# Fifteen small loads, of 1 to 15 rows, put beside a saturated load stream

## The chip, the cores and the metric

One core of one Trainium2 chip. The metric is the device time of one execution, in microseconds (us). A program on one core is timed in several runs; the profile comes from one more execution. Its "span" runs from the first to the last instruction and is some 1.8 to 2.1 us shorter than the device time.

## The reference, cut to what matters

```python
# B, S, D, W = 4, 4096, 4096, 64;  x is (4, 4096, 4096) fp32, w is (4096, 4096) fp32
def reference(x, w, offsets):
    for b in range(B):
        o = int(offsets[b])
        results.append(x[b, o:o+W] @ w)          # four windows of 64 rows, one weight matrix
    return np.stack(results).astype(np.float32)   # (4, 64, 4096)
```

The weights are 67.1 MB of fp32 and the windows 4.2 MB. Every byte is read once: 71.3 MB.

## The kernel before

POOL (GpSimd) issues nearly all loads, as its queue can turn fp32 into fp16 on the way. The weights come in blocks of up to four times 128 rows into three rotating buffers `wc`, then in a "tail" of 1 MB pieces (counted as fp16):

```python
blocks = [(0, 1), (1, 1), (2, 4), (6, 4), (10, 4), (14, 4), (18, 3), (21, 3)]
k_tail = 24
wc_pool = ctx.enter_context(tc.tile_pool(name="wc", bufs=3))
x_pool = ctx.enter_context(tc.tile_pool(name="xp", bufs=1))
...
for k0, r in blocks[2:]:
    t = wc_pool.tile([P, R_MAX * N], fp16, name="wc", tag="wc")
    nc.gpsimd.dma_start(
        out=t[:, : r * N],
        in_=w[k0 * P : (k0 + r) * P, :].rearrange("(p r) n -> p (r n)", r=r),
    )
```

For each block PE multiplies all eight column groups for both pairs of windows, and DVE adds each result to the accumulator; the program is in manual order, so each engine runs its instructions as they are written:

```python
whole_rows([0, 1], range(8), True)
for k0, r in blocks[2:-1]:
    whole_rows(range(k0, k0 + r), range(8), False)
```

At the end the second half of the output goes out through two hardware queues, ACT's and SP's. SP does nothing between its one load at the start and these stores:

```python
q = [nc.scalar, nc.sync]
for h in range(2):
    ...
    for g in range(G):
        for j in js:
            add_out(4 * g + j, g, ng * n_sub + j)
        store(q[g], g, c0, c0 + NG // 2)
```

## Time and profile before

| | before |
|---|---|
| time, median of 2 runs | 182.29 us (182.23 to 182.35) |
| span of the profiled execution | 180.6 us |
| share of the span on the chain that ended last | DMA 63%, PE 26% |
| bytes read | 71.30 MB |
| last load of weights landed, PE starts its last pieces | 164.84 us |

How to read it: the chain says that the end was waiting for data for most of the time, and the bytes read, over the time in which they were read, say at what rate. The lines, with their reading, stand in the prediction.

### The profile page before, as it was taken

How to read it: one execution, taken by the hardware profiler on the slowest of the kernel's cores; microseconds unless marked ns; L12 is line 12 of the kernel's file. 1: busy time of each engine (PE TensorE's matmuls, PEld its weight loads, DVE VectorE, ACT ScalarE, POOL GpSimd, SP SyncE). 2: the span in 40 equal slices, each digit the busy share in tenths (PEclk: the TensorE clock that was granted, in tenths of full speed). 3: DMA queues.
4: the chain of work that ended last, by engine and by line, in shares of the span. 5: the costliest groups of instructions: out<-in, count | busy, mean ns of one | idle time of the engine just before them, and what ended most of it. 6: DMA issues, size and time to landing. Idle time of an engine off the chain costs nothing.

```text
span 180.6 us, 1505 instructions
## 1 busy us (share of the span) xinstructions
PE 125.7 (70%) x576; PEld 58.1 (32%) x576; DVE 80.5 (45%) x120; ACT 16.5 (9%) x23; POOL 14.5 (8%) x29
## 2 busy tenths in 40 slices
PE   0000779504999399808995699999399999987900
PEld 0000774101444144303442244444044444433400
DVE  0000657500578278802876168899374000820460
ACT  2412446500000000000000000000000000400000
POOL 4600000000000100000001000050500100020000
PEclk9999999965799999996999889999879999999996
DMA  5999989999999899999989989999999999999994
GB/s 178 321 256 212 281 181 196 236 232 232 225 218 218 174 210 234 236 218 232 210 181 203 245 191 245 194 239 196 191 212 213 215 216 214 212 216 206 370 419 196
DMA packets 4952, 40.98 MB, mean 227 GB/s; under 512 B 466, under 2 KB 466, under 8 KB 3282
## 3 DMA queue, kind: packets, MB, share of 16 engines
q0 software_dynamic: 4080, 36.70, 93.8%
q1 hardware_dynamic: 432, 2.10, 3.2%
q10 hardware_dynamic: 434, 2.10, 2.8%
q8 instruction: 4, 0.07, 0.1%
q14 instruction: 2, 0.02, 0.0%
HBM read 71.30 MB, written 4.19 MB: 418 GB/s over the span
## 4 chain that ended last, share of the span: by engine, by line
DMA 63%; PE 26%; issue 3%; DVE 2%; POOL 1%; POOLq 1%; DVEq 0%
DMA wc<-in_w_dram 63%; PE bank L144 26%; DVE acc L154 2%; POOL wc L108 1%; POOLq L70 1%; POOL xrow L77 0%; DVEq L251 0%; POOL identity masks.py:197 0%; POOLq L77 0%; POOL w L66 0%; POOLq masks.py:199 0%; DVEq L154 0%; POOLq L240 0%
## 5 line engine op out<-in xcount | busy, mean ns | idle before, releaser
L144 PE MATMUL bank<-wc,xT 128*128 128x512 f16 x480 | 111.6, 396 | 26.2 <-DMA wc<-in_w_dram 26.2
L154 DVE TENSOR_TENSOR acc<-acc,bank 128x512 f32<-128x512 f32 x100 | 67.0, 686 | 70.7 <-PE bank L144 70.0
L144 PEld LDWEIGHTS <-xT 128*128 128x128 f16 x512 | 51.5, 101 | 93.1 <-DMA wc<-in_w_dram 26.7
L130 PE MATMUL bank<-identity,xrow 128*128 128x128 f16 x64 | 7.1, 312 | 20.0 <-DMA xrow<-in_x_dram 20.0
L139 DVE CAST xT<-bank 128x512 f16<-128x512 f32 x8 | 5.5, 692 | 21.9 <-PE bank L130 21.9
L130 PEld LDWEIGHTS <-xrow 128*128 128x128 f16 x64 | 6.7, 149 | 20.2 <-issue 20.2
L200 ACT COPY tmp<-bank 128x512 f32<-128x512 f32 x4 | 2.1, 600 | 119.9 <-PE bank L144 119.9
L89 POOL DMA_DIRECT2D wc<-in_w_dram x6 | 3.2, 542 | 88.2 <-PE bank L144 88.2
L108 POOL DMA_DIRECT2D wc<-in_w_dram x10 | 6.7, 683 | 36.0 <-PE bank L144 26.4
L144 PE MATMUL bank<-w,xT 128*128 128x512 f16 x32 | 7.2, 382 | 0.0
L169 DVE COPY acc<-bank 128x512 f32<-128x512 f32 x8 | 5.5, 692 | 1.4 <-PE bank L144 1.2
L141 ACT CAST xT<-bank 128x512 f16<-128x512 f32 x8 | 4.7, 586 | 8.2 <-PE bank L130 8.2
L171 ACT COPY acc<-bank 128x512 f32<-128x512 f32 x8 | 4.7, 586 | 2.3 <-PE bank L144 2.3
L189 POOL DMA_DIRECT2D out_dram<-acc x2 | 1.1, 534 | 18.1 <-DVE acc L205 18.1
L205 DVE TENSOR_TENSOR acc<-acc,tmp 128x512 f32<-128x512 f32 x4 | 2.5, 681 | 0.0
L63 ACT CAST w<-acc 128x2048 f16<-128x2048 f32 x1 | 1.9, 1897 | 4.9 <-DMA acc<-in_w_dram 4.9
L77 POOL DMA_DIRECT2D xrow<-in_x_dram x4 | 2.1, 523 | 2.1 <-issue 2.1
L62 ACT CAST w<-acc 128x2048 f16<-128x2048 f32 x1 | 1.9, 1897 | 3.0 <-DMA acc<-in_w_dram 3.0
L62 ACT ACT_TABLE_LOAD x1 | 1.3, 1283 | 1.8 <-PEq L240 1.8
L66 POOL DMA_DIRECT2D w<-in_w_dram x1 | 0.7, 660 | 0.8 <-POOLq L240 0.8
masks.py:199 POOL TENSOR_SCALAR_AFFINE_SELECT identity<-identity 128x128 f16<-128x128 f16 x1 | 0.3, 287 | 0.1
masks.py:197 POOL MEMSET identity<- 128x128 f16 x1 | 0.2, 223 | 0.0
(4 smaller groups left out, 0.4 us busy)
## 6 DMA issues: line engine op xcount, KB each, us to landing
wc<-in_w_dram POOLq DMA_DIRECT2D x4, 4096.0 KB, 48.2
wc<-in_w_dram POOLq DMA_DIRECT2D x7, 1024.0 KB, 27.5
wc<-in_w_dram POOLq DMA_DIRECT2D x2, 3072.0 KB, 36.1
xrow<-in_x_dram POOLq DMA_DIRECT2D x4, 512.0 KB, 14.7
out_dram<-acc POOLq DMA_DIRECT2D x2, 1024.0 KB, 14.5
acc<-in_w_dram SPq DMA_DIRECT2D x1, 1024.0 KB, 5.3
w<-in_w_dram POOLq DMA_DIRECT2D x1, 1024.0 KB, 12.2
acc<-in_w_dram ACTq DMA_DIRECT2D x1, 1024.0 KB, 11.5
```

Of the source, the lines that this page charges most:

```text
L62: nc.scalar.copy(out=w_one[0][:, :NG], in_=w0_32[:, :NG])
L77: nc.gpsimd.dma_start(out=x16[g][m * WIN : (m + 1) * WIN, :], in_=x[b][bass.ds(o, WIN), :],)
L89: nc.gpsimd.dma_start(out=t[:, : r * N], in_=w[k0 * P : (k0 + r) * P, :].rearrange("(p r) n -> p (r n)", r=r),)
L108: nc.gpsimd.dma_start(out=t[:, pos : pos + n * wd].rearrange("p (t n) -> p t n", t=n), in_=w[ki * P : (ki + n) * P, ng * NG + c0 : ng * NG ...
L130: nc.tensor.matmul(out=ps[t][:, i * P : (i + 1) * P], lhsT=x_cols(g, 4 * t + i), rhs=identity[:], start=True, stop=True,)
L139: nc.vector.tensor_copy(out=dst, in_=ps[t][:])
L141: nc.scalar.copy(out=dst, in_=ps[t][:])
L144: nc.tensor.matmul(out=ps[bank][:], lhsT=xT[g][:, kt * P : (kt + 1) * P], rhs=rhs, start=start, stop=stop,)
L154: nc.vector.tensor_add(out=dst, in0=dst, in1=ps[bank][:])
L169: nc.vector.tensor_copy(out=acc[g][:, c * NT : (c + 1) * NT], in_=ps[bank][:])
L171: nc.scalar.copy(out=acc[g][:, c * NT : (c + 1) * NT], in_=ps[bank][:])
L205: nc.vector.tensor_add(out=dst, in0=dst, in1=tmp[2 * g + j // 2][:])
```

## The change

Its intent, as far as the code tells it: to see what a handful of tiny transfers, issued from an otherwise idle queue in the middle of a saturated stream, costs. The loaded data are used by nothing. Each load has n rows of 16 fp32 numbers, 64 bytes a row, for n from 1 to 15. The memset before them, on DVE, is what holds them in place: SP waits for it.

```diff
     tmp = [acc_pool.tile([P, NT], fp32, name=f"tmp{i}") for i in range(4)]
+    small = x_pool.tile([16, 16 * 16], fp32, name="small")
     acc = [acc_pool.tile([P, N], fp32, name=f"acc{g}") for g in range(G)]
 ...
     for k0, r in blocks[2:-1]:
         whole_rows(range(k0, k0 + r), range(8), False)
+        if k0 == 10:
+            nc.vector.memset(small[:], 0.0)
+            for n in range(1, 16):
+                nc.sync.dma_start(
+                    out=small[:n, 16 * n : 16 * n + 16], in_=w[0:n, 16 * n : 16 * n + 16]
+                )
```

## The prediction

> **What bounds the kernel now.** I read the page first, then the chain that ended last, then busy time by stretches, then the two timelines where the change lands. The page of the profile, its parts 1 to 4:
>
> ```profile
> span 180.6 us, 1505 instructions
> ...
> DMA  5999989999999899999989989999999999999994
> ...
> q0 software_dynamic: 4080, 36.70, 93.8%
> q1 hardware_dynamic: 432, 2.10, 3.2%
> q10 hardware_dynamic: 434, 2.10, 2.8%
> ...
> HBM read 71.30 MB, written 4.19 MB: 418 GB/s over the span
> ...
> DMA 63%; PE 26%; issue 3%; DVE 2%; POOL 1%; POOLq 1%; DVEq 0%
> ```
>
> The span is 180.6 us of the 182.29 us measured. The DMA row stands at 8 or 9 tenths in every slice but the first and last. Of the packet time, 93.8% of 16 engines' span is queue 0, the loads and two stores that POOL issues; the two hardware queues (q1 is SP's, q10 is ACT's) have 6% between them. The chain is 63% DMA. The chain of waits in order of time, from the middle on:
>
> ```profile
> 59.54 41.55 DMA wc<-in_w_dram
> ...
> 101.13 26.05 PE bank L144 x112
> ...
> 127.47 1.39 POOL wc L108 x2
> 128.86 35.94 DMA wc<-in_w_dram
> ...
> 164.84 5.36 PE bank L144 x24
> 170.20 1.35 DVE acc L154 x3
> ```
>
> Columns are start, length, what. PE's 26.05 us from 101.13 is there only because the chain stepped to the buffer that PE freed for the last loads. The following 35.94 us of DMA say the same thing as the total: 71.30 MB are read from 0.9 us to the landing at 164.8 us, 71.30 MB / 163.9 us = 435 GB/s. After that landing come 7 us of matmuls, the adds and the stores, which wait for nothing else. Busy time by stretch shows whether the stream ever runs dry:
>
> ```profile
> core 0: us, PE busy (x) PEld busy (x) DVE busy (x) ACT busy (x) POOL busy (x), PEclk, DMA share, GB/s
> 43.00:97.00 54.00, 45.44 (x192) 19.49 (x192) 32.06 (x47) 0.00 (x0) 1.06 (x2) 0.93 1.00 215
> 98.00:101.00 3.00, 0.00 (x0) 0.00 (x0) 0.10 (x1) 0.00 (x0) 0.20 (x1) 1.00 0.72 153
> 108.00:127.00 19.00, 19.00 (x89) 8.53 (x87) 17.07 (x27) 0.00 (x0) 2.83 (x4) 1.00 1.02 218
> 133.00:163.00 30.00, 29.34 (x137) 13.24 (x136) 9.46 (x15) 2.06 (x4) 2.16 (x4) 1.00 1.06 214
> ```
>
> The last two columns are the DMA share and GB/s written into SBUF; the loads read fp32 and write fp16, so what is read is twice that: 430, 436 and 428 GB/s in the three long stretches. One rate through blocks in long pieces and the tail in short ones: the DMA engines are the wall. The 0.72 in the three-microsecond stretch is no hole: packets of 2.4 us are counted where they start, and the neighbouring microseconds make up for it (97 to 98 us alone counts 1.82). Anything that takes time on the busiest of the 16 DMA engines before 164.8 us moves the end; anything on SP, and short work in a gap of DVE, does not.
>
> **What the Trainium skill says, and whether this trace agrees.**
> (1) "DMA: Bandwidth & Descriptors", Issuing engines are not separate DMA queues: loads issued by any engine run on the same 16 DMA engines and interleave. Agrees: two loads of the same 1024 KB, one from SP and one from ACT, were issued 0.5 us apart and took 5.3 and 11.5 us to land.
> (2) The same page, Why a DMA increments its semaphore by 16 and not by 1: a hardware load is spread over the largest k of at most 16 that divides the slowest dimension of both sides, on the lowest-numbered k engines, each writing one completion. So n rows (n from 2 to 15) would use engines 0 to n-1. The trace has one small load to compare, the offsets on ACT's queue. SP's queue has 432 packets: three transfers of 128 rows and 3 x 16 completions. ACT's has 434, the same and two more: one data packet, one completion, so k = 1. The case n = 11 or 13 no run shows yet.
> (3) The same page, Queues, rings and completion order: an engine takes turns between its queues a packet at a time, and a completion write lands only after all earlier writes of that engine, whatever their queue. The first half agrees with the interleaving in (1). What the second half costs the other queue is the rival below.
> (4) "HBM Reference", Latency: an access takes 0.2 us on average, 2 us under high load. I use it only to size that rival; the trace of before does not show it by itself.
>
> **The change part by part.** It removes nothing. It adds one memset, fifteen loads on SP's queue, and a buffer of 1 KB per partition, used by nothing that is computed. The order on each engine is the program's own, so the memset comes after the sixteen adds of the block that starts at 10 and before those of the next. The timeline there:
>
> ```profile
> 97.41 0.69 DVE L154 TENSOR_TENSOR acc<-acc,bank 128x512 f32<-128x512 f32 x1 [0.18 <-PE bank L144]
> 97.67 0.53 POOL L89 DMA_DIRECT2D wc<-in_w_dram  x1 [20.55 <-PE bank L144]
> ...
> 101.13 4.33 PE L144 MATMUL bank<-wc,xT 128*128 128x512 f16 x12 [3.76 <-DMA wc<-in_w_dram]
> 102.21 0.69 DVE L154 TENSOR_TENSOR acc<-acc,bank 128x512 f32<-128x512 f32 x1 [4.11 <-PE bank L144]
> ```
>
> *The memset.* The last add of that block ends at 97.41 + 0.69 = 98.10 us, and DVE then stands idle for 4.11 us until the first group of the next block. An add of 512 columns takes 0.69 us on DVE; half the columns, 256, at no better pace is 0.34 us (an estimate). It fits twelve times over: cost 0. POOL's issue of the next block load at 97.67 is through at 98.20, 0.1 us into the memset, and the data it calls for is queued behind a whole block anyway.
>
> *Issuing on SP.* What SP does in the whole kernel, by its timeline:
>
> ```profile
> 0.87 0.38 SPq L59 DMA_DIRECT2D acc<-in_w_dram  x1
> 172.08 2.72 SPq L189 DMA_DIRECT2D out_dram<-acc  x2
> ```
>
> Between 0.87 and 172.08 us it does nothing. At the 0.38 us that its one load took to issue, fifteen are 5.7 us: from about 98.5 to 104.2 us if nothing holds them. The framework may make later ones wait for the landing of earlier ones, to use a completion counter again. In the worst case every data packet and every completion waits for one turn behind a packet of the big stream: 30 turns. The trace's own packet records give 2.43 us for the packets of four-row blocks and 1.83 us for those of three-row blocks. Four turns to about 109 us, ten to 128 us, and the rest behind the tail's packets of 0.32 us: all done before 135 us. SP is needed at 172. Cost 0.
>
> *The DMA engines.* 1 + 2 + ... + 15 = 120 rows of 64 bytes, 7.7 KB beside 71.3 MB: the bytes are nothing. The packets count. With k = n, engine 0 gets fifteen data packets and fifteen completions, engine 14 one of each, engine 15 none. In the packet records, the 32-byte packet of the offsets took 7 ns, and a completion 9 ns on SP's queue and 22 ns (median) on POOL's. A data packet of 64 bytes I put at 7 to 14 ns (an estimate). Engine 0: 15 x (7 + 9) = 0.24 us to 15 x (14 + 22) = 0.54 us. The wc landings wait for the slowest engine; if that is engine 0, the end moves by this, otherwise by less, down to 0.
>
> *The end.* SP's closing waits may have some more completion counters to look at, all long reached: I allow 0.1 us. The new buffer moves the addresses of those after it by 1 KB; nothing in the profile depends on that.
>
> Sum: 0 + 0 + (0 to 0.54) + (0 to 0.1) us, so 0 to 0.64, middle 0.3: 182.6 us.
>
> **The rivals.**
> *Wholly hidden.* Engine 0 is not the slowest, and its delay is absorbed by the lag of another. For it: the skill's count puts all the load on low engines. Against: the views don't show single DMA engines. Time 182.3, which cannot be told from my own number without many rounds.
>
> *A bubble at each completion or each change of queue.* If an engine had to let its earlier writes land, with nothing else under way, before each of fifteen completions, engine 0 would lose about 0.2 us each by (4): 15 x 0.2 = 3 us, and the time 185.3; at the 2 us of a loaded memory it would be 30 us and 212. Against it: the tail's loads have one completion per sixteen packets on each engine, and POOL's issues that waited for their landings (130.42, 135.32, 140.37 us) are 4.90 and 5.05 us apart, while sixteen packets of 0.324 us are 5.18 us. So a completion leaves no hole in its own queue. Also, while ACT's 1 MB load and POOL's first loads share the engines, the packet records add up to 434 GB/s read, not less than POOL's queue alone (427). What speaks for it: all these were large packets, and fifteen tiny ones on one engine are not seen anywhere in before. I give it 6% for more than 3.65 us.
>
> *SP's queue backs up into its last stores.* Worked out above: it would have to last 74 us, over twice the worst case. Under 1%.
>
> *Faster.* Nothing is removed and no wait is broken; a gain could only be chance.
>
> **Range and chances.** Before ran at 182.23 and 182.35, its profiled execution at 182.56: 0.2 us of noise around a shift of 0 to 0.64. That gives 182.1 to 183.2; I stretch the upper end to 183.8 for small bubbles (0.1 us times fifteen on engine 0). Two per cent is 3.65 us, six times my largest sum, so the verdict is the same with 0.93; slower 0.06 by the bubbles, faster 0.01.
>
> **What would show it right or wrong.** In the changed profile: SP's queue with 120 more data packets and 120 completions, so about 672 packets in place of 432 (fewer if k is smaller for some); the memset on DVE just after 98 us inside an idle gap; the first matmul of the next block still near 101.1 us; fifteen SP issues from about 98.5 us; a last wc landing at 164.8 to 165.5 us; from there to the end some 16 us as before. Wrong if that landing is 3 us or more later with the DMA share in 98 to 135 us lower than 0.97 (bubbles), if a wait of SP for its own small loads reaches 172 us (backing up), or if the matmuls after 101 us wait longer for wc with no later bytes.

## The result, and the profile after

The changed kernel took 182.57 us (182.4 to 182.74, 2 runs) against 182.29 us; the ratio is 1.0011, with a 95% interval of 0.9991 to 1.0031. "Same" was right, and the 182.6 of the prediction too; what has to be found out is whether it was right for its reasons, as 0.28 us is not more than the noise.

The page of the changed kernel, the parts that answer to those shown of before:

```profile
span 180.9 us, 1525 instructions
...
DMA  5999988999999899999998989898999999999994
...
q0 software_dynamic: 4080, 36.70, 93.7%
q1 hardware_dynamic: 672, 2.11, 3.3%
...
HBM read 71.31 MB, written 4.19 MB: 417 GB/s over the span
...
DMA 60%; PE 27%; issue 3%; DVE 2%; another core or an unknown queue 2%; POOL 1%; POOLq 1%; DVEq 0%
```

SP's queue q1 went from 432 to 672 packets: 240 more, 120 rows and 120 completions, as the rule of one engine per row has it, for 11 and 13 as for the rest. POOL's queue is as it was, packet for packet. In the chain of waits in order of time (start, length, what), the end is this:

```profile
116.26 10.55 PE bank L145 x48
...
128.49 36.41 DMA wc<-in_w_dram
...
164.94 5.35 PE bank L145 x24
170.29 1.35 DVE acc L155 x3
```

PE takes up the last pieces at 164.94 us, against 164.84 before. The timeline where the change lands (start, length, engine, line, operation, with the idle time before it in brackets):

```profile
97.42 0.69 DVE L155 TENSOR_TENSOR acc<-acc,bank 128x512 f32<-128x512 f32 x1 [0.17 <-PE bank L145]
...
98.10 0.27 DVE L178 MEMSET small<- 16x256 f32 x1
98.40 27.23 SPq L180 DMA_DIRECT2D small<-in_w_dram  x15
...
101.11 13.99 PE L145 MATMUL bank<-wc,xT 128*128 128x512 f16 x64 [3.72 <-DMA wc<-in_w_dram]
102.18 0.69 DVE L155 TENSOR_TENSOR acc<-acc,bank 128x512 f32<-128x512 f32 x1 [3.81 <-PE bank L145]
```

The memset starts in the nanoseconds in which the last add ends, and DVE still has 3.81 us of idle time after it; the block's first matmul starts at 101.11 us, against 101.13. The surprise is the SP line: fifteen issues stretch over 27 us, from 98.40 to 125.6. Its waits, and the first 5 us of the same timeline cut off at 103 us:

```profile
SPq L196 <- DVE acc L155: 44.7, 2, 42.8
SPq L180 <- DMA small<-in_w_dram: 22.4, 7, 4.3
SPq L258 <- DMA out_dram<-acc: 4.5, 4, 1.2
SPq L196 <- DMA small<-in_w_dram: 3.7, 1, 3.7
```

```profile
98.40 2.59 SPq L180 DMA_DIRECT2D small<-in_w_dram  x8
```

The columns of the first are total us, times, longest. Eight loads go out in a row, 2.59 us; each of the other seven waits for an earlier small load to land, 22.4 us in all. So there are eight completion counters for this purpose, used in turn. This will matter at the end. The last line is SP's first store, which waits 3.7 us for the counter of a small load, straight after the last issue: that is over by about 129.4 us, 40 us before SP is needed, so the prediction's sign of backing up didn't show.

Why does a load of at most 15 rows need 4 us and more? The trace's DMA records (no view prints them singly) show the first data packet at 103.1 us, its completion at 104.9, the next load's data at 106.8, and so on, mostly 1.81 to 1.83 us apart on one engine: one packet, data or completion, for each turn behind a packet of the big stream, which took 1.83 us in this block. (Near 114 and 128.7 us, where the stream goes over to its next load, some come close together.) The last small packet started at 132.6 us. This is the worst case of the prediction's paragraph on SP, and it is what happened; the 40 us to SP's store at 172 were enough.

### The profile page after: what moved, and what is told of

It is laid out like the page before. It is cut to its first block, busy times and chain, and to the rows that moved or that the text cites. A ratio compares the mean times of both kernels' runs of the same rounds, so it can differ in the third digit from the quotient of the medians. Undisturbed runs are those within 1.5% of the kernel's fastest.

```text
span 180.9 us, 1525 instructions
## 1 busy us (share of the span) xinstructions
PE 127.7 (71%) x576; PEld 58.4 (32%) x576; DVE 80.8 (45%) x121; ACT 16.5 (9%) x23; POOL 14.5 (8%) x29
## 4 chain that ended last, share of the span: by engine, by line
DMA 60%; PE 27%; issue 3%; DVE 2%; another core or an unknown queue 2%; POOL 1%; POOLq 1%; DVEq 0%
DMA wc<-in_w_dram 60%; PE bank L145 27%; DVE acc L155 2%; POOL wc L109 1%; POOLq L71 1%; POOL xrow L78 0%; DVEq L258 0%; POOL identity masks.py:197 0%; POOLq L78 0%; POOL w L67 0%; POOLq masks.py:199 0%; DVEq L155 0%; POOLq L247 0%
## 5 line engine op out<-in xcount | busy, mean ns | idle before, releaser
L145 PE MATMUL bank<-wc,xT 128*128 128x512 f16 x480 | 113.4, 400 | 24.5 <-DMA wc<-in_w_dram 24.5
```

The lines of the kernel that those rows point to most:

```text
L145: nc.tensor.matmul(out=ps[bank][:], lhsT=xT[g][:, kt * P : (kt + 1) * P], rhs=rhs, start=start, stop=stop,)
```

## The experiments

Twelve kernels were run, in three calls, each call with its own runs of before on the same chip: 4 to 6 runs of each, 9 to 11 of before. Medians, with ratios:

| run | this, us | before, us | ratio | 95% interval |
|---|---|---|---|---|
| same_again | 182.61 | 182.26 | 1.0014 | 1.0001 to 1.0027 |
| memset_only | 182.34 | 182.26 | 1.0000 | 0.9988 to 1.0012 |
| four_times | 183.08 | 182.26 | 1.0039 | 1.0026 to 1.0052 |
| rows_127 | 182.43 | 182.26 | 1.0003 | 0.9990 to 1.0016 |
| loads_57 | 182.65 | 182.44 | 1.0017 | 1.0003 to 1.0030 |
| loads_12 | 182.75 | 182.44 | 1.0016 | 1.0002 to 1.0030 |
| wide_127 | 193.10 | 182.44 | 1.0615 | 1.0560 to 1.0669 |
| wide_128 | 183.20 | 182.44 | 1.0045 | 1.0030 to 1.0061 |
| loads_17 | 182.32 | 182.33 | 1.0000 | 0.9987 to 1.0014 |
| both_127 | 184.39 | 182.33 | 1.0117 | 1.0102 to 1.0133 |
| mid_127 | 185.09 | 182.33 | 1.0153 | 1.0139 to 1.0166 |
| late60 | 195.98 | 182.33 | 1.0749 | 1.0733 to 1.0766 |

All gave the correct result.

### First call: is there a shift, and is it the packets?

**same_again** is the changed kernel unedited.

> The changed kernel once more, in five rounds, to narrow the shift. Three theories of what the fifteen loads cost. PACKETS: each small packet takes its own recorded time (24 ns for 64 bytes, 22 ns for a completion) from the stream of engine 0, and engine 0 sets the end: 15 x 46 ns = 0.69 us, ratio 1.004. HIDDEN: engine 0 has slack, or the small packets fit into time the stream doesn't use: ratio 1.000. BUBBLE: each completion or change of queue also leaves a hole, 0.1 us or more each: 15 x 0.1 = 1.5 us or more, ratio 1.008 or more.

1.0014, with an interval that just leaves out 1.000: a shift of about a quarter of a microsecond, a third of what the small packets' recorded times add up to on engine 0. BUBBLE is out: a hole of even 0.1 us per completion would be six times the shift. Between PACKETS and HIDDEN it doesn't decide.

**memset_only**:

```diff
         if k0 == 10:
             nc.vector.memset(small[:], 0.0)
-            for n in range(1, 16):
-                nc.sync.dma_start(...)
```

> The memset and the buffer stay, the fifteen loads are left out. All theories: 182.3 us as before, ratio 1.000 within 0.2%, as the 0.27 us of the memset lie in a DVE gap of 4 us. If the shift of the change is found here again, it came from the memset or the moved addresses and not from the loads.

1.0000. The memset and the moved addresses cost nothing; what shift there is belongs to the loads.

**four_times**:

```diff
-            for n in range(1, 16):
+            for i in range(60):
+                n = i % 15 + 1
                 nc.sync.dma_start(
-                    out=small[:n, 16 * n : 16 * n + 16], in_=w[0:n, 16 * n : 16 * n + 16]
+                    out=small[:n, 16 * i : 16 * i + 16], in_=w[0:n, 16 * i : 16 * i + 16]
                 )
```

(and `small` with 64 x 16 columns.)

> Sixty loads in place of fifteen, same shapes, same place. PACKETS: 60 x 46 ns = 2.8 us, 185.1 us, ratio 1.015. HIDDEN: 182.3 to 182.6, ratio below 1.003. BUBBLE: 6 us or more, ratio 1.03 or more. Turns: if engine 0 gives each small packet one turn behind a packet of the big stream, as the records of the changed kernel suggest (a small packet every 1.82 us on engine 0 while the stream moves 1.83 us packets), 120 turns are 16 of 1.83 us and 104 of about 0.35 us: the last small packet near 165 us, just before SP's last stores at 172, so no backing up.

0.82 us by the medians: between PACKETS and HIDDEN, and near neither. The last small completion started at 159.4 us, expected near 165, and SP's stores were issued at 172.17, as with fifteen loads: no backing up. But in the chain of waits PE takes up its last pieces at 164.94 us, exactly as in the changed kernel with fifteen. The stream doesn't know of the 45 further loads. So the 0.4 us that sixty cost over fifteen in the span (181.3 against 180.9) arise after the stream, and I looked there; this is where the theory CLOSING of the second call comes from.

**rows_127**:

```diff
-            for n in range(1, 16):
-                nc.sync.dma_start(...)
+            nc.sync.dma_start(out=small[:127, 0:16], in_=w[0:127, 0:16])
```

(and `small` with 128 partitions.)

> One load of 127 rows of 64 bytes in place of the fifteen: by the skill's rule 127 has no divisor of at most 16 but 1, so all 127 data packets and one completion should lie on one engine; then SP's queue shows 432 + 128 = 560 packets. PACKETS: 127 x 24 ns = 3.0 us, 185.3 us, ratio 1.017. HIDDEN: 182.3 to 182.6. BUBBLE by completion: one hole, 182.5; BUBBLE by change of queue: 127 x 0.1 = 13 us or more. Turns: at one packet a turn the load ends near 165 us; if several of its rows go in one turn, far earlier.

The queue's line on the page, and the chain of waits:

```profile
q1 hardware_dynamic: 560, 2.11, 3.3%
```

```profile
128.82 35.76 DMA wc<-in_w_dram
...
164.62 5.35 PE bank L145 x24
```

560 packets: 127 rows and one completion, so one engine carried them all. They came one per turn, mostly 308 ns apart in the tail of the stream, up to 160.6 us. By their records 2.97 us of that engine's time; measured, 0.17 us by the medians, not clear of noise, and a PE that takes up its last pieces sooner than in before.

The end alone doesn't say whether the packets cost nothing or whether that engine had time in hand; the stream's own completion records do. (The records don't number the engines; "engine 0" is here a name for the one that carries the small load.) In the tail an engine finishes its share of a 1 MB piece every sixteen large packets, and its completion is recorded. In before these completions are 4.895 us apart, on most engines alike. In rows_127 those that stand among the small packets are 4.960 us apart, seventeen small packets between two of them (133.33, 138.29, 143.25 us and so on): 3.8 ns for a small packet, 0.49 us for 127. PACKETS is out: a record's 24 ns is not time taken from the stream. And engine 0 does have time in hand: it finishes the piece before these first of the sixteen, at 128.37 us, when the last one finishes at 129.78. A piece counts as landed with the last engine, so the first 1.4 us that engine 0 loses can't show.

### Second call: the closing waits, and real bytes

After the last store SP goes through the completion counters one after the other before the kernel may end. No view prints these waits singly; the trace's instruction records do. Their starts in us, on SP:

```
before        174.85 174.92 174.98 175.04 175.10 | 175.97 177.23 178.48 179.72 |                                    end 180.61
fifteen       175.00 175.06 175.12 175.19        | 176.25 177.48 178.73 179.82 | 179.88 179.94                      end 180.86
sixty         175.11 175.17                      | 177.84 179.09 180.02        | 180.08 180.14 180.20 180.29 180.37  end 181.28
```

The middle group ends as a store lands; the left ones had been satisfied before, the right ones too, but they are only looked at after the last landing. Each takes 60 to 90 ns of SP. What SP waited for in this phase can be seen in its waits (total us, times, longest) of the sixty loads; the same line of the changed kernel, L258 above, has four waits with a longest of 1.2:

```profile
SPq L259 <- DMA out_dram<-acc: 4.9, 4, 2.6
```

The order is that of the eight counters, and the counter of a store is set by how many hardware loads came before it. Seven hardware transfers in before use seven of them, and the last store has the last. Every load more moves the four stores on by one. With N loads added, the waits left behind the last landing should be, for N = 1, 9, 17, 57: none; for 15: two; for 12 and 60: five.

**loads_57** and **loads_12** are four_times with `range(57)` and `range(12)`.

> The sixty loads less the last three: 57. Theory CLOSING (new, from the traces so far): the loads don't slow the stream at all; they turn the order in which SP's closing waits go through the eight completion counters of hardware loads. A wait that comes after the last store's landing costs about 62 ns; the changed kernel has 2 of them behind the landing, the sixty loads 5, before and the 127 rows none. With 57 loads (57 = 8 x 7 + 1, the place of the single load of 127 rows) none should be left behind: 182.3 to 182.5, ratio below 1.002, where sixty took 1.0039. Theory PACKETS (a cost per small packet, some 12 ns of the 46 seen): 57/60 of the sixty's 0.71 us: 182.95, ratio 1.0037.

> Only the first twelve loads (1 to 12 rows). CLOSING: 12 = 8 + 4, the same place as sixty, so five waits of 62 ns or more behind the landing: 182.6 to 182.9, ratio 1.002 to 1.0035, at least as much as the fifteen (1.0014). PACKETS: 12 x 12 ns = 0.15 us, 182.4, ratio 1.0008, less than the fifteen.

By the clock the two are alike, 1.0017 and 1.0016 (0.21 and 0.31 us by the medians), though the one has almost five times the loads of the other: a cost per load doesn't give that. But 12 came out just under the ratio I gave. And 57, for which CLOSING leaves nothing, took 182.65 us where 182.3 to 182.5 were expected (before itself took 182.44); its ratio is under the 1.002 I gave, but its interval leaves out 1.000. So CLOSING isn't all of the shift there, and the clock can't put the two in order. The trace is sharper. Taken from it, for every run, the time from the end of SP's last store packet to the end of the span:

| waits behind the landing | runs: us |
|---|---|
| 0 | before 1.26, memset_only 1.26, rows_127 1.28, loads_57 1.28, loads_17 1.27, mid_127 1.25, wide_127 1.25, wide_128 1.27 |
| 2 | changed kernel 1.40, same_again 1.39 |
| 5 | loads_12 1.58, four_times 1.63, late60 1.64 |
| 7 | both_127 1.68 |

Fourteen executions, in order, without an exception: 1.25 to 1.28 us, and 60 to 75 ns more for each wait. It doesn't go with the number of loads: twelve loads stand with sixty, 57 with none.

**wide_127** and **wide_128**:

```diff
-            for n in range(1, 16):
-                nc.sync.dma_start(...)
+            nc.sync.dma_start(out=small[:127, :], in_=w[0:127, 0:512])     # wide_127
+            nc.sync.dma_start(out=small[:128, :], in_=w[0:128, 0:512])     # wide_128
```

(and `small` as 128 x 512.)

> One load of 127 rows of 2048 bytes, all on engine 0 as the 127 small rows were. About 80 ns a row (half of the 159 ns that 4096 bytes take in the store's records), so 10.2 us of engine 0's time. If the 3 us of 127 small packets vanished because engine 0 had slack against the other engines, the end moves by 10.2 less that slack: up to 7 us, 189, ratio 1.04. If they vanished because small packets fit into time that the engine doesn't use between the stream's packets, real bytes will not: the full 10 us, 192.5, ratio 1.056. If neither (the end isn't set by the engine that ends last), 182.5.

> One row more: 128 rows of 2048 bytes, so by the skill's rule spread over all sixteen engines, 8 rows each: 8 x 80 ns = 0.64 us on each engine, 182.9, ratio 1.0035, whichever engine sets the end; SP's queue with 432 + 128 + 16 = 576 packets. If the rule of k doesn't hold, the same as 127 rows.

The chain of waits of the two, first 127 rows, then 128:

```profile
129.02 45.37 DMA wc<-in_w_dram
...
174.43 5.35 PE bank L145 x24
```

```profile
130.12 35.31 DMA wc<-in_w_dram
...
165.47 5.35 PE bank L145 x24
```

One row more, and the end comes 9 us sooner. 127 rows sit on one engine, and PE takes up the last pieces at 174.43 us, 9.6 us later than before. (Their 260 KB are 9.8 us at the expectations' 26.5 GB/s, which is 8 KB in 309 ns; in the tail of before an engine starts one every 307.) The time was 192.04 to 194.81 us in four runs; the profiled one is of the faster kind, and why the others took 2 us more I can't say. 128 rows are spread: 0.64 us were expected, PE is 0.63 us later, the time 0.76. That 9.6 is so close to 9.8 us is not a sign that engine 0 has no slack: its completions are now 6.429 us apart, 90 ns more for each small packet, 11.5 us for 127 rows if all cost that (an estimate). Some 1.9 us of it didn't reach the end, about the lead seen in rows_127. The 64-byte packets of rows_127 vanished because they were 0.5 us of work and not 3 us, and because the lead covers that.

### Third call: how small is free, the order of counters again, and the case that hurts

**loads_17** is four_times with `range(17)`.

> Seventeen loads, the fifteen and two more of 1 and 2 rows: 17 = 8 x 2 + 1, the place of 57 and of the single load. CLOSING: no closing wait is left behind the last store's landing, so from that landing's last packet to the span's end about 1.27 us as before, against 1.40 us with fifteen: two loads more, an end 0.13 us sooner; the time 182.3 to 182.6, ratio below 1.0015 (0.13 us is too little for the clock of five rounds to show; the trace decides). PACKETS or BUBBLE: a little more than fifteen.

182.32 against 182.33 us, ratio 1.0000: two loads more than the changed kernel and, if anything, sooner, though the interval is as wide as the shift that is looked for. The trace has no closing wait behind the landing and 1.27 us to the end.

**both_127**:

```diff
+            nc.sync.dma_start(out=small[:127, 0:16], in_=w[0:127, 0:16])
+            nc.scalar.dma_start(out=small[:127, 16:32], in_=w[0:127, 16:32])
```

(in place of the fifteen.)

> The 127 rows of 64 bytes twice, once from SP and once from ACT, both after the memset, so two more queues take turns on engine 0: 254 data packets, 254 x 24 ns = 6.1 us by their records; by their bytes 254 x 64 = 16 KB at the 26.5 GB/s at which the engine moves 8 KB packets, 0.6 us. If the small packets of one queue were hidden in some slack of a few us, twice as many should come out of it: up to 3 us, ratio 1.017. If a small packet costs only its bytes: 182.5 to 183.2, ratio 1.001 to 1.004.

```profile
128.23 38.00 DMA wc<-in_w_dram
...
166.27 5.35 PE bank L145 x24
```

2.06 us. CLOSING has its part: this pair leaves seven waits behind the landing, 0.42 us. PE takes up the last pieces 1.43 us later than in before, which neither the bytes (0.6 us) nor the records (6.1 us) give. The records show what happened turn by turn: on each turn of engine 0 one packet of each of the two queues, and turns of 331 ns (median, after 131 us) where rows_127 with one packet per turn had 308. Without any small packet, a 1 MB piece of the tail, sixteen turns per engine, landed every 4.90 and 5.05 us: 306 and 316 ns a turn. So the first small packet of a turn hardly lengthens it (3.8 ns, as above), the second adds some 20 ns, near its recorded time. By the completions of engine 0, 5.309 us apart, a pair costs 24 ns, 3.1 us for 127 pairs (an estimate, as above); less the lead of 1.4 us or somewhat more, that is about what PE shows. My expectation that one rule would hold for both was wrong.

**mid_127** is rows_127 with 128 columns, 512 bytes a row.

> 127 rows of 512 bytes on engine 0, between the 64 bytes that cost nothing to be seen and the 2048 bytes that cost 10.7 us. By bytes: 127 x 512 / 26.5 GB/s = 2.45 us, 184.8, ratio 1.013. By their share of what 2048 bytes cost, 10.7 / 4 = 2.7 us, ratio 1.015. If a piece up to some size fits into unused time of the engine, clearly less than 2 us, ratio below 1.010.

```profile
129.04 38.55 DMA wc<-in_w_dram
...
167.63 5.36 PE bank L145 x24
```

2.76 us, PE 2.8 us later: 22 ns a row, a little over the 19 ns of its bytes (127 x 512 bytes are 2.45 us). But here too the lead of engine 0 hides a part: its completions are 5.469 us apart, 34 ns for each small packet, 4.3 us for 127. Put together ("hidden" is the estimated loss less what PE shows):

| 127 rows on engine 0 | its loss per row (or pair), ns | times 127, us (estimate) | PE later than before, us | hidden, us |
|---|---|---|---|---|
| 64 bytes | 3.8 | 0.5 | -0.2 | all |
| 64 bytes, twice | 24 | 3.1 | 1.4 | 1.7 |
| 512 bytes | 34 | 4.3 | 2.8 | 1.5 |
| 2048 bytes | 90 | 11.5 | 9.6 | 1.9 |

So two things are at work: a lone 64-byte packet in a turn costs next to nothing, and whatever engine 0 loses, some 1.5 to 1.9 us of it is covered by the slower engines. What sizes between 64 and 512 bytes cost wasn't measured.

**late60** moves the memset and sixty loads behind the adds of the first output half:

```diff
+    nc.vector.memset(small[:], 0.0)
+    for i in range(60):
+        n = i % 15 + 1
+        nc.sync.dma_start(
+            out=small[:n, 16 * i : 16 * i + 16], in_=w[0:n, 16 * i : 16 * i + 16]
+        )
     ng = order[1]
     k_fine = n_k - n_fine
```

(and the block at `k0 == 10` goes; `small` has 61 x 16 columns.)

> The sixty loads moved to the end: the memset after the last adds of the first output half (near 159 us), the loads on SP from there, in front of SP's last two stores. The rival of the prediction that I gave under 1%: SP's queue backing up into its stores. Sixty loads landing one per 0.4 to 1 us, with eight completion counters, keep SP until 185 to 200 us, where its first store was issued at 172; the end comes some 8 us after that: 192 to 208, ratio 1.05 to 1.14. If SP doesn't hold its stores back behind its loads' landings, or they land much faster near the end: 182.5 to 185.

SP's timeline, and one line of its waits:

```profile
0.87 0.38 SPq L60 DMA_DIRECT2D acc<-in_w_dram  x1
159.04 29.73 SPq L212 DMA_DIRECT2D small<-in_w_dram  x60
188.89 0.85 SPq L190 DMA_DIRECT2D out_dram<-acc  x2
```

```profile
SPq L212 <- DMA small<-in_w_dram: 5.2, 9, 1.6
```

The sixty take SP from 159.04 to 188.8 us, about 0.5 us each, and its two stores, issued from 172.08 in before, leave at 188.89. The end is 13.65 us later. PE takes up its last pieces at 164.64 us, so the stream is as fast as ever. The same sixty loads cost 0.8 us in the middle and 13.7 at the end. The number came out as expected, the reason only in part: waits for small loads to land make up 5.2 us of the 29.7, one more wait for a store 3.2 us. Most of it is the issuing itself, 0.295 us a load (median) and what lies between.

## Why the prediction was right or wrong

**The total and the verdict** were right: 182.57 for 182.6, "same" at 0.93.

**What bounds the kernel** was right and is now shown: some 11 us of work on one DMA engine (wide_127) moved the end by 10.7 us; the memset and SP's issuing, off the engines, moved nothing that was measured.

**The memset, SP's issuing, the turns** were right: memset 0.27 us for an estimated 0.34, in the gap named; an issue 0.30 us (median) for 0.38; 672 packets; all small packets gone by 132.6 us for "before 135". The loads did not go out by 104 us; they ran into the worst case that the text had set aside beside it, and its sum held (its first four turns took 1.83 us and not 2.43, but the first packet went only at 103.1).

**The term that was mis-sized** is *The DMA engines*: 0.24 to 0.54 us "if that is engine 0" on which the landings wait, "otherwise by less, down to 0". The stream moved by 0.10 us in the profile and 0.01 us in the second one (PE takes up its last pieces at 164.94 and 164.85 us); over all profiles with small loads of 64 bytes from SP alone this start lies between 164.62 and 164.94, so neither is clear of noise. The step that failed is taking a packet's record for time of its engine. The records turned out longer than guessed (24 ns for 64 bytes, not 7 to 14), which by the prediction's sum would be 0.69 us; but a lone one costs 3.8 ns. Records overlap: the page's DMA share runs over 1.00 in this stream, which I had before my eyes, and the prediction's own sixteen packets of 0.324 us, 5.18 us, landed every 4.90 to 5.05. Besides, the landings don't wait for engine 0, which in rows_127 is 1.4 us ahead of the last: the "down to 0" was the case.

**The other mis-sized term** is *The end*: 0.1 us allowed for further counters "to look at, all long reached". The mechanism was named, and it cost 0.13 to 0.14 us in the two profiles of the changed kernel, about half of the quarter of a microsecond; what I had not seen is that it depends on the number of loads modulo 8 and can be zero. With 17 loads, where it is zero, no shift was measured (1.0000), but with 57, where it is zero too, 1.0017 was: the rest of the shift isn't explained. That the sum of 0.3 us came out right is partly luck: its parts were the other way round, the larger from the closing, little or none from the engines.

**The rivals.** *Wholly hidden* is what the stream did, and the reason given, that engine 0 is not the slowest, is borne out by the lead of 1.4 us; beside it stands that the packets cost less than their records. *A bubble* of 0.1 us or more is refuted by same_again, and by rows_127, with 127 changes of queue and no cost. *SP backing up* didn't happen in the change; late60 shows that it can happen, there mostly by the time that issuing takes, and that the place in the program kept it away.

**Left open:** why the first small packet in a turn is nearly free and the second is not; which of the sixteen engines are the slow ones, and why; 0.2 us in the times of loads_57, with no closing wait to explain them (the spans of the same rounds are 0.2 us longer too, 180.7 against 180.5 by the medians); and in the profile of four_times 0.2 us between the stream's end and the last store's packet that closing waits don't explain.

## What to carry to other kernels

Small loads from an idle hardware queue can ride beside a saturated stream at next to no cost, as long as few packets and bytes land on any one engine and no critical store stands behind them on the same queue; count their landing in turns of the big stream's packets, not in their own length. Watch the row count: 127 rows of 2 KB cost 10.7 us where 128 rows cost 0.8. Before an unchanged end is read as "no cost", look whether the loaded engine had a lead to lose: the spacing of its completions showed a cost that the end hid. And before a shift of a tenth of a per cent is put down to data movement, look at what the kernel does after its last landing: here it was a matter of which counter the last store happened to get.

## What the Trainium skill lacked or had wrong

- "DMA: Bandwidth & Descriptors", Queues, rings and completion order: it speaks of packets of some 9 to 17 descriptors that are drained before the engine turns to another queue. Here the turn was one data piece or one completion: 127 rows on one engine came mostly 308 ns apart, one behind each packet of the stream, and a load of 1 row needed two turns of 1.82 us each. (Whether a record of the trace is a packet in the page's sense, no run shows.)
- The same page, Why a DMA increments its semaphore by 16 and not by 1: the rule of k held (120 completions for 1 to 15 rows; 1 for 127 rows; 16 for 128). It doesn't say what an odd row count costs a kernel bound by its loads: 10.7 us for 127 rows of 2 KB against 0.8 us for 128.
- The same page, Specifications: 512 bytes as the least size for full rate suggests that 64-byte rows are dear for their bytes. Beside a full stream they were not: on the engine that carries them a lone 64-byte row cost 3.8 ns and one of 512 bytes, eight times as long, 34 ns. No run here times them without the stream.
- No page that I found has the closing waits: SP goes through the completion counters in a fixed order, and each wait left behind the last landing costs 60 to 75 ns (1.26 us from the last packet to the end with none, 1.68 with seven).
